# The last pair's queries and keys moved through DRAM in two parts

## The chip, the cores and the metric

The kernel runs on one core of a Trainium2 chip. The metric is the device time of one execution in microseconds (us), the median of several runs. TensorE (PE) does matmuls, VectorE (DVE), ScalarE (ACT) and GpSimd (POOL) the elementwise work, and nearly all DMAs are issued from the queue of SyncE (SP), in the order of that queue.

## The reference

Two layers on a sequence of 512 tokens with 1024 features, all in float32. Layer A (the one that the change touches) is a dilated sliding-window attention with three groups (dilation 1, 4 and 16), layer B a neighbourhood attention on a grid of 8 x 64 tokens.

```python
hn = rms_norm(x, norm_gain[i])
proj = hn @ w_in                          # q, k, v for 3 groups x 16 heads of 64, and a gate
...
    q = rms_norm(qkv[:, :, g, 0], q_gain[g])      # per head
    k = rms_norm(qkv[:, :, g, 1], k_gain[g])
    v = qkv[:, :, g, 2]
    o, lse = dilated_group_attention(q, k, v, t5_bias, dilation, reach)
...
alpha = jax.nn.softmax(jnp.stack(lses), axis=0)   # merges the three groups
y = jnp.sum(alpha[..., None] * jnp.stack(outs), axis=0) * jax.nn.silu(gate)
x = x + y @ w_out
```

## The kernel before, in words

**Tiling.** Work in a layer goes by pairs of heads, `hc` = 0 to 7. For each pair of layer A, `main_a` projects, with three float32r matmuls for each float32 product (weights and activations are split into a high and a low part: `wh`/`wl`, `hn_h`/`hn_l`):

- "rawk": dilated keys and values of groups 1 and 2 (keys normed into the last 256 of the 768 columns of each quarter of `rq`, called `rawq` in the trace);
- "rawq": three groups' queries and group 0's near keys (the first 512 columns of each quarter);
- group 0's values, and the gate.

For pairs 0 to 6 "rawk" comes first; for pair 7 "rawq" comes first, then "rawk", the gate of pair 6, the values and the gate of pair 7, and then the output product over all eight pairs (`out_product`, `acc<-y,wh` in the trace). Two pieces of weights (`wraw`, 512 KB each, four buffers) are loaded ahead by SP; ACT copies each into `wh` (L142), DVE or POOL makes `wl` (L150).

**How queries and keys are moved.** The scores need each head's 64 features on partitions, so every pair goes through a transposition: DVE norms (L336) and transposes 32x32 blocks in place (`turn_raw`, L591); `move_q` (L686) writes all 768 columns of the four quarters to a DRAM tile `qd` (1.5 MB, one DMA, L692), and four reads of 32 partitions each bring them back as `qt` (L699). Then `split_q` (L747) has ACT spread group 0's keys into `k0` (L753) and the queries of the three groups into places of their own (L750, L753). The dilated keys are used from `qt` directly. The scores (`log<-k,rawk` for group 0, `log<-qt,q` for the dilated groups, L238) follow, 16 and 32 matmuls for each of the four token blocks (two blocks in a half of the pair).

The scores of pair 6 that have gone through softmax make the same kind of trip (`tr` to `td` to `pt`: L882, L886), as do group 0's values (`vv` to `vd` to `vv`: L641, L645). The biases of a pair are loaded as `e` (L845).

**What sets the order.** PE's order is written out: `run` walks through `main` (projections and output product), and between its steps through `side` (attention), which yields delays in a modelled clock of PE's work (`clock`), in ns. `yield "wait", key, delay` lets `side` go on when the clock is `delay` past the moment at which `key` was stamped; `later_on(delay, job)` puts a job, often a DMA, at a later point of the same clock. So delays in the code are places in the program, not times on the chip: on the chip each engine runs its own list in order and waits for what an instruction needs. DMAs marked `keep_in_program_order` stand in SP's list where the clock put them. Each DMA on SP also takes one of eight semaphores in turn, so it waits for the landing of the one issued eight before it.

For pair 7, `q_a` (L680) waits for the "rawk" stamp and `Q7` = 9500, then calls `move_q`; `land` waits to `Q7` + 10000 and calls `split_q`; `attn_a` then yields 3500 and emits the first scores.

Of the kernel before, what the change touches and what calls it, by code (L numbers as in the profile page):

```python
# [13 lines left out]
F32 = mybir.dt.float32  # L14
# [8 lines left out]
P = 128  # L23
# [3 lines left out]
NHC = 8  # L27
# [4 lines left out]
EXT = S + 64  # L32
LINE = 384 + 2 * 448
W5 = 5 * 32
Q7 = 9500
RUN = 6 * 64
EB = 8 * W5

# [22 lines left out]
def tile_hybrid_encoder(  # L61
# [11 lines left out]
    nc = tc.nc  # L73
# [8 lines left out]
    dr = ctx.enter_context(tc.tile_pool(name="dr", bufs=1, space=DRAM))  # L82
# [29 lines left out]
    def slot(k, name, dtype):  # L112
        return big.tile([P, 2 * S], dtype, tag="y%d" % k, name=name)
# [137 lines left out]
    def later_on(delay, job):  # L251

        timers.append((clock[0] + delay, job))
        timers.sort(key=lambda t: t[0])
# [123 lines left out]
    def row_scale(ssq):  # L378

        rsqrt(nc.vector, rs_n, ssq, 4, 1.0 / D)  # L380
# [48 lines left out]
    def square_a(k):  # L429
        nc.scalar.activation(x_of(k), x_of(k), AF.Square)  # L430
# [72 lines left out]
    st = {}  # L503
    pq = wk.tile([P, 4096], F32, tag="pt", name="pt", bufs=1)
    rk = wk.tile([P, 4096], F32, tag="rawk", name="rawk", bufs=1)
    rq = wk.tile([P, 3072], F32, tag="rawq", name="rawq", bufs=1)
# [163 lines left out]
    def q_tiles(hc):  # L670


        if ("q", hc) not in st:
            st["q", hc] = (
                wk.tile([P, 4, 6, P], F32, tag="q12", name="qt", bufs=1),
                wk.tile([P, EXT], F32, tag="k0", name="k0", bufs=1),
            )
        return st["q", hc]

    def q_a(hc):  # L680

        yield "wait", *((("rawq", hc), 8000) if hc < NHC - 1 else (("rawk", hc), Q7))
        del st["rawq", hc]
        move_q(hc)

    def move_q(hc):  # L686

        d = dr.tile([4, P, 768], F32, name="qd", tag="qd", bufs=2)
        left = [4]

        def write():
            tc.keep_in_program_order(nc.sync.dma_start(d.rearrange("a p x -> p a x"), rq.rearrange("p (a x) -> p a x", a=4)))  # L692
            stamp["q", hc] = 0

        def read(a):
            qt, _ = q_tiles(hc)
            dst = qt[32 * a : 32 * a + 32].rearrange("k t f x -> k t (f x)")
            src = d[a].rearrange("(t k) x -> k t x", t=4)
            tc.keep_in_program_order(nc.sync.dma_start(dst, src))  # L699
            left[0] -= 1  # L700

        later_on(600, write)

        def land():
            for a in (0, 2, 1, 3):
                later_on(6500 if hc < NHC - 2 else 5000, partial(read, a))
            if hc < NHC - 1:
                yield "wait", ("rawk" if hc < NHC - 2 else "rawq", hc + 1), 0
            else:
                yield "wait", ("rawk", hc), Q7 + 10000  # L710
            assert not left[0]
            split_q(hc, *q_tiles(hc))
            yield

        st["land", hc] = land

# [24 lines left out]
    def split_q(hc, qt, k0):  # L741
        src = qt[:, :, 3, :].rearrange("p s (j i) -> p s i j", j=4)
        dst = k0[:, 64:EXT].rearrange("p (i s j) -> p s i j", s=4, j=4)
        tc.keep_in_program_order(scaled(dst, src, 0))
        both = slot(hc, "q12", F32)
        areas = st["areas", hc] = rk[:, 3072 : 3072 + S], both[:, :S], both[:, S:]
        for g, to in enumerate(areas):  # L747
            src = qt[:, :, g, :].rearrange("p s (x r) -> p s x r", r=8)
            dst = to.rearrange("p (x s r) -> p s x r", s=4, r=8)
            tc.keep_in_program_order(scaled(dst, src, g) if g else nc.scalar.copy(dst, src))  # L750

    def scaled(dst, src, g):
        return nc.scalar.activation(dst, src, AF.Copy, scale=gk[:, g : g + 1])  # L753
# [140 lines left out]
    def attn_a(hc):  # L894
# [115 lines left out]
        if hc < NHC - 1:  # L1010
            for u in range(2):
                if u == 0:
                    yield "wait", ("rawk" if hc < NHC - 2 else "rawq", hc + 1), 6500
                elif hc < NHC - 3:
                    yield "wait", ("open", hc + 1), 2500
                elif hc == NHC - 3:
                    yield "wait", ("rawq", hc + 1), 9000
                else:
                    yield "wait", ("rawq", hc + 1), 23200
                turned = turner(512)  # L1020
                turners.append(turned)
                for hd, t, pr in scores(u):
                    turned.put(pr, 512, 256 * hd + 64 * (t % 2), 128)
                send = partial(turned.send, pq[:, 2048 * u : 2048 * u + 2048], *((6000, 500) if u else (8500, 1200)))
                later_on(7000 + 2000 * u, send)
                if pending and u == 0:
                    yield 7500
                    pending.pop(0)()
                    yield 0
                if u == 0:  # L1030
                    yield "half"
            pending.append(lambda: put_y(hc, weigh(), True, False))
        else:
            for u in range(2):
                yield 3500 if u == 0 else 600
                held = scores(u)
                if u:
                    stamp["ya", "turned"] = 0
                yield 3200
                if pending:  # L1040
                    yield "wait", ("gate", hc - 1), 18500
                    pending.pop(0)()
                    yield
                for args in held:
                    turn_p(*args)
                    yield
            yield "wait", ("v", hc), 0
            put_y(hc, weigh(), True, True)
            stamp["ya", "last"] = 0
            yield  # L1050
# [271 lines left out]
    def side():  # L1322
        for k in range(KT):
            norm(0, k, x_of(k))
            if k:
                square_a(k - 1)
            stamp["na", k] = 0
            if k == 4:
                gains()
            yield 1000  # L1330
        square_a(KT - 1)
        for k in range(1, KT):
            yield 1300
            nc.vector.tensor_add(x_of(0), x_of(0), x_of(k))
        yield 1500
        row_scale(row_sums(x_of(0)))
        yield 2500
        bias_lines()
        later_on(21000, lambda: st.__setitem__(("e", 0), bias_a(0)))
        yield 2500  # L1340
        scales_a()
        first_out()
        stamp["rs", "a"] = 0
        halves = []
        for hc in range(NHC):
            if hc < NHC - 1:
                yield from q_a(hc)
                if hc:
                    yield from halves.pop(0)
                yield from st.pop(("land", hc))()  # L1350
                half = attn_a(hc)
                for v in half:
                    if v == "half":
                        if hc == 0:
                            later_on(12500, bias_rows)
                        if hc in (4, 5):
                            for n in range(2):
                                later_on(9000 + 3500 * n, st["rows"].pop())
                        halves.append(half)
                        break  # L1360
                    yield v
            else:
                gap[0] = cycle((500, 500, 700))
                yield from halves.pop(0)
                yield from q_a(hc)
                yield from st.pop(("land", hc))()
                yield from attn_a(hc)
        yield from residual(xg, 0)
        yield from residual(xg, 4)
        stamp["ya", KT - 1, "y"] = 0  # L1370
        yield "wait", ("x", KT - 1), 800
        for f in range(KT):
            square_b(f)
            yield 600
        yield 4500
        row_scale(row_sums(st.pop("ssq")))
        stamp["rs", "b"] = 0
        yield 5000
        nc.scalar.mul(rs_half, spread(), 0.5)
        stamp["rs", "all"] = 0  # L1380
        for job, hc, delay in B_PLAN:
            yield "wait", ("b", "start"), delay
            if job == "scores":
                yield from side_b(hc)
                continue
            if hc == NHC - 1:
                yield "wait", ("back", hc), 0
                yield from residual(xm_d, 0)
            yield "wait", ("back", hc), 3500
            if hc == NHC - 2:  # L1390
                stamp["yb", "turned"] = 0
            pending.pop(0)()
            if hc == NHC - 1:
                stamp["yb", "last"] = 0
            yield
            if hc == NHC - 1:
                yield from residual(xm_d, 4)
# [105 lines left out]
```

## Time and profile before

| | |
|---|---|
| median of 3 runs | 813.52 us (813.51 to 813.93) |
| the profiled execution | 815.16 us, span 813.4 us |
| busy, share of the span | PE 795.8 us (98%), DVE 531.3 (65%), ACT 444.4 (55%), POOL 221.2 (27%) |
| chain that ended last | PE 82%, DVE 8%, DMA 5%, ACT 2% |
| DMA | 178.43 MB, 219 GB/s on average |
| layer A's last pair | first scores at 512.43 us, output product from 490.25 us |

In the rows of the trace, times are us from the span's start. A row of a timeline has start, duration, engine, line of the code, operation, output <- inputs, and in brackets how long the engine was idle before it and what ended that. `wraw<-in_w` is a load of weights. "Granted clock" is the share of full speed that PE's throttle allowed; "DMA share" is the mean busy share of the core's 16 DMA engines.

### The profile page before, as it was taken

The page shows a single profiled execution, that of the slowest core. Times are in us where ns is not written, and L with a number is a line of the kernel's source. Part 1 is how long each engine was busy: PE and PEld are TensorE (multiplying, and loading weights), DVE is VectorE, ACT ScalarE, POOL GpSimd, SP SyncE. Part 2 cuts the span into 40 slices and gives each one's busy share as a digit, 9 for nine tenths or more (in the row PEclk, how much of TensorE's full clock was granted, in tenths as well). Part 3 has the DMA queues.
Part 4 walks back from the last instruction along what each step waited for, and adds up shares of the span by engine and source line. Part 5 has one row for each costly group of instructions (what it writes and reads, how often), then busy time and mean ns, then how long its engine had stood idle before and what let it go on. Part 6 is the DMA issues. An engine that isn't in the chain of part 4 may idle for free.

```text
span 813.4 us, 17707 instructions
## 1 busy us (share of the span) xinstructions
PE 795.8 (98%) x6690; PEld 652.2 (80%) x6690; DVE 531.3 (65%) x1409; ACT 444.4 (55%) x936; POOL 221.2 (27%) x349
## 2 busy tenths in 40 slices
PE   9999999999999999999999995799999999999998
PEld 7888888888888888888888884678888888878887
DVE  7474675675675675675676784348565788796844
ACT  7442745645645645744746662545535665657721
POOL 3242432332432432432433131111130405020010
PEclk9999999999999999999999999799999999999999
DMA  8579588878977987987978589327745797799564
GB/s 288 167 203 261 145 240 245 252 202 251 267 218 221 271 240 220 273 270 204 267 266 236 183 233 276 95 63 287 182 155 172 218 229 223 217 258 279 160 157 177
DMA packets 99590, 178.43 MB, mean 219 GB/s; under 512 B 16752, under 2 KB 53632, under 8 KB 99504
## 3 DMA queue, kind: packets, MB, share of 16 engines
q1 hardware_dynamic: 99360, 177.03, 74.4%
q8 instruction: 53, 0.87, 0.4%
q10 hardware_dynamic: 144, 0.26, 0.1%
q14 instruction: 33, 0.27, 0.1%
HBM read 132.82 MB, written 52.70 MB: 228 GB/s over the span
## 4 chain that ended last, share of the span: by engine, by line
PE 82%; DVE 8%; DMA 5%; ACT 2%; issue 1%; POOL 0%; SPq 0%; ACTq 0%; DVEq 0%; POOLq 0%
PE acc L238 73%; PE log L238 4%; PE o L238 4%; DMA wraw<-in_w 2%; DVE wl L150 1%; DVE rawq L336 1%; DMA qt<-qd 1%; DMA vv<-vd 1%; DMA qd<-rawq 1%; DMA vv<-bd 1%; DVE rawq L591 1%; PE busy L402 1%; DVE p L942 1%; ACT p L1262 0%; DVE na L129 0%
## 5 line engine op out<-in xcount | busy, mean ns | idle before, releaser
L238 PE MATMUL acc<-wh,hn_h 128*128 128x512 f32 x704 | 277.5, 395 | 0.0
L238 PE MATMUL acc<-wh,hn_l 128*128 128x512 f32 x704 | 273.7, 389 | 0.0
L238 PE MATMUL acc<-wl,hn_h 128*128 128x512 f32 x704 | 273.7, 389 | 0.0
L142 ACT CAST wh<-wraw 128x512 fp32r<-128x512 f32 (+1 forms) x257 | 157.2, 615 | 192.2 <-PE acc L238 165.2
L150 DVE TENSOR_TENSOR wl<-wraw,wh 128x512 fp32r<-128x512 f32 (+2 forms) x186 | 139.1, 749 | 142.0 <-ACT wh L142 140.2
L150 POOL TENSOR_TENSOR wl<-wraw,wh 128x512 fp32r<-128x512 f32 (+1 forms) x72 | 97.0, 1348 | 242.8 <-ACT wh L142 182.6
L238 PEld LDWEIGHTS acc<-wh,hn_h 128*128 128x128 f32 x704 | 132.4, 188 | 31.4 <-issue 3.8
L238 PEld LDWEIGHTS acc<-wh,hn_l 128*128 128x128 f32 x704 | 132.2, 188 | 28.0
L238 PEld LDWEIGHTS acc<-wl,hn_h 128*128 128x128 f32 x704 | 132.2, 188 | 26.8 <-POOL wl L150 0.3
L316 POOL TENSOR_TENSOR sq<-rawq 128x256 f32<-128x256 f32 (+1 forms) x80 | 57.7, 729 | 123.4 <-ACT rawq L554 109.8
L238 PE MATMUL acc<-y,wh 128*128 128x512 f32 (+1 forms) x272 | 82.6, 387 | 1.0 <-DVE mn L954 0.6
L965 ACT ACTIVATE p<-p,mn 128x512 f32<-128x512 f32 (+1 forms) x64 | 44.8, 702 | 60.6 <-DVE mn L954 60.6
L238 PE MATMUL acc<-hn_h,wh 128*128 128x512 f32 x192 | 75.4, 393 | 0.1
L238 PE MATMUL acc<-hn_h,wl 128*128 128x512 f32 x192 | 74.9, 390 | 0.0
L238 PE MATMUL acc<-hn_l,wh 128*128 128x512 f32 x192 | 74.8, 389 | 0.0
L317 DVE TENSOR_REDUCE ss<-sq 128x4 f32<-128x256 f32 (+1 forms) x96 | 47.7, 506 | 35.0 <-POOL sq L316 30.3
L238 PEld LDWEIGHTS acc<-y,wh 128*128 128x128 f32 x272 | 49.5, 190 | 11.0 <-PE log L238 0.8
L238 PE MATMUL acc<-y,wl 128*128 128x512 f32 (+1 forms) x136 | 51.7, 380 | 0.0
L336 DVE TENSOR_TENSOR rawq<-rawq,rs 128x256 f32<-128x256 f32 (+1 forms) x96 | 47.1, 551 | 2.5 <-POOL rs L134 2.2
L873 DVE STREAM_TRANSPOSE tr<-p 128x512 f32<-128x512 f32 x56 | 38.9, 706 | 11.9 <-ACT p L789 11.7
L554 ACT ACTIVATE rawq<-acc,rs_n 128x512 f32<-128x512 f32 (+1 forms) x76 | 46.1, 613 | 0.5
L789 ACT ACTIVATE p<-p,mn 128x512 f32<-128x512 f32 (+1 forms) x64 | 44.4, 701 | 2.4 <-DVE mn L788 2.3
(127 smaller groups left out, 908.0 us busy)
## 6 DMA issues: line engine op xcount, KB each, us to landing
wraw<-in_w SPq DMA_DIRECT2D x121, 512.0 KB, 5.6
td<-tr SPq DMA_DIRECT2D x14, 1024.0 KB, 7.4
pt<-td SPq DMA_DIRECT2D x56, 256.0 KB, 4.9
qd<-rawq SPq DMA_DIRECT2D x8, 1536.0 KB, 7.6
qt<-qd SPq DMA_DIRECT2D x32, 384.0 KB, 6.6
tdb<-tb SPq DMA_DIRECT2D x8, 768.0 KB, 6.1
pt<-tdb SPq DMA_DIRECT2D x32, 192.0 KB, 5.7
eb<-eb_d SPq DMA_DIRECT2D x32, 160.0 KB, 5.7
```

What stands on the lines that cost most here:

```text
L142: nc.scalar.copy(h, raw)
L150: eng.tensor_sub(l, raw, h.bitcast(F32))
L238: nc.tensor.matmul(o, l, r, **kw)
L316: nc.gpsimd.tensor_mul(to, v, v)
L317: nc.vector.tensor_reduce(ss[:, i * ns : (i + 1) * ns], sq.rearrange("p (a b) -> p a b", b=64), axis=AX.X, op=ALU.add)
L336: m = nc.vector.tensor_mul(v, v, by)
L402: nc.tensor.matmul(busy, wide(P), wide(S), start=True, stop=True)
L554: nc.scalar.activation(dst, src, AF.Copy, scale=rs_n[:, i : i + 1])
L591: tc.keep_in_program_order(nc.vector.transpose(x, x))
L789: nc.scalar.activation(pr, pr, AF.Copy, scale=mn[:, 3:4])
L873: nc.vector.transpose(dst, src[:, :n].rearrange(order, b=4, k=32, **({"g": 2} if apart else {})))
L965: nc.scalar.activation(row, row, AF.Exp, bias=mn[:, 1:2], scale=-1.0, accum_out=mn[:, 2:3])
```

## The change

For the last pair alone, `move_last` takes the place of `move_q`. The queries (and near keys), 512 of each quarter's 768 columns, are written when their own norm is through, read back in four reads after the next projection, and spread by `split_q` earlier. The dilated keys, 256 columns, are written and read back by themselves later: `Q7` is now 13000 and their reads stand 4500 behind that. The half-finished attention of pair 6 (`halves.pop(0)`) now runs after `q_a` of pair 7, and the pause ahead of the last pair's first scores is 6000 where it was 3500.

```diff
-Q7 = 9500
+Q7 = 13000
...
     def q_a(hc):
-        yield "wait", *((("rawq", hc), 8000) if hc < NHC - 1 else (("rawk", hc), Q7))
+        yield "wait", ("rawq", hc), 8000
         del st["rawq", hc]
-        move_q(hc)
+        (move_q if hc < NHC - 1 else move_last)(hc)
...
-            if hc < NHC - 1:
-                yield "wait", ("rawk" if hc < NHC - 2 else "rawq", hc + 1), 0
-            else:
-                yield "wait", ("rawk", hc), Q7 + 10000
+            yield "wait", ("rawk" if hc < NHC - 2 else "rawq", hc + 1), 0
...
+    def move_last(hc):
+
+        d = dr.tile([4, P, 768], F32, name="qd", tag="qd", bufs=2)
+        queries, keys = slice(0, 512), slice(512, 768)
+
+        def write(x):
+            src = rq.rearrange("p (a x) -> p a x", a=4)[:, :, x]
+            tc.keep_in_program_order(nc.sync.dma_start(d.rearrange("a p x -> p a x")[:, :, x], src))
+
+        def read(x):
+            for a in (0, 2, 1, 3):
+                dst = q_tiles(hc)[0][32 * a : 32 * a + 32].rearrange("k t f x -> k t (f x)")[:, :, x]
+                src = d[a].rearrange("(t k) x -> k t x", t=4)[:, :, x]
+                tc.keep_in_program_order(nc.sync.dma_start(dst, src))
+
+        later_on(600, partial(write, queries))
+
+        def land():
+            yield "wait", ("rawk", hc), 2000
+            read(queries)
+            yield "wait", ("rawk", hc), 12500
+            split_q(hc, *q_tiles(hc))
+            yield "wait", ("rawk", hc), Q7
+            write(keys)
+            yield "wait", ("rawk", hc), Q7 + 4500
+            read(keys)
...
-                yield 3500 if u == 0 else 600
+                yield 6000 if u == 0 else 600
...
                 gap[0] = cycle((500, 500, 700))
+                yield from q_a(hc)
                 yield from halves.pop(0)
-                yield from q_a(hc)
                 yield from st.pop(("land", hc))()
```

What this does to the engines' lists is shown at three places. In the changed kernel, line numbers behind the new function are 26 higher. `x4` means four such instructions in a row; sizes are partitions and elements.

First place, SP's list where pair 6's first half of scores goes out to DRAM (`td`), during pair 7's projections. Before:

```order
L882 DMA td<-tr 128x4x512
L845 DMA e_5442<-l_d 128x2x256
L845 DMA e_5443<-l_d 32x4x224 x4
L886 DMA pt<-td 32x4x512 x4
L202 DMA wraw<-in_w 128x1024 x2
```

And now:

```order
L908 DMA td<-tr 128x4x512
L721 DMA qd<-rawq 128x4x512
L871 DMA e_5444<-l_d 128x2x256
L871 DMA e_5445<-l_d 32x4x224 x4
L912 DMA pt<-td 32x4x512 x4
L202 DMA wraw<-in_w 128x1024
L727 DMA qt<-qd 32x4x512 x4
L202 DMA wraw<-in_w 128x1024
```

The queries' write stands right behind `td`, their four reads behind the first of the two loads of weights.

Second place, SP's list that follows, where pair 6's second half goes out and the keys of pair 7 are through their norm. Before:

```order
L882 DMA td<-tr 128x4x512
L202 DMA wraw<-in_w 128x512
L886 DMA pt<-td 32x4x512
L692 DMA qd<-rawq 128x4x768
L202 DMA wraw<-in_w 128x1024
L641 DMA vd<-vv 128x4x128
L202 DMA wraw<-in_w 128x768
L699 DMA qt<-qd 32x4x768 x4
L886 DMA pt<-td 32x4x512 x3
L645 DMA vv<-vd 32x4x128 x4
```

And now:

```order
L908 DMA td<-tr 128x4x512
L202 DMA wraw<-in_w 128x512
L721 DMA qd<-rawq 128x4x256
L912 DMA pt<-td 32x4x512 x4
L202 DMA wraw<-in_w 128x1024
L727 DMA qt<-qd 32x4x256 x4
L641 DMA vd<-vv 128x4x128
L202 DMA wraw<-in_w 128x768
L645 DMA vv<-vd 32x4x128 x4
```

The keys' write has moved ahead of all four `pt` reads (one stood before it, three behind the reads of `qt`); the keys' reads stand behind those four and one load of weights; the values' `vd` has moved behind the keys' reads.

Third place, ACT's list between the last two gates of layer A (`eg<-gt` is a gate's tanh, `gt<-acc` the copy of a gate out of PSUM) and the last pair's first softmax. Before:

```order
L613 ACTIVATE eg<-gt 128x512
L142 CAST wh<-wraw 128x512 x4
L608 COPY gt<-acc 128x512
L613 ACTIVATE eg<-gt 128x512
L142 CAST wh<-wraw 128x512 x3
L753 ACTIVATE k_5716<-qt,gk 128x4x32x4
L750 COPY rawk<-qt 128x4x16x8
L753 ACTIVATE q_5771<-qt,gk 128x4x16x8 x2
```

And now:

```order
L613 ACTIVATE eg<-gt 128x512
L142 CAST wh<-wraw 128x512 x2
L779 ACTIVATE k_5619<-qt,gk 128x4x32x4
L776 COPY rawk<-qt 128x4x16x8
L779 ACTIVATE q_5706<-qt,gk 128x4x16x8 x2
L142 CAST wh<-wraw 128x512 x2
L608 COPY gt<-acc 128x512
L613 ACTIVATE eg<-gt 128x512
L142 CAST wh<-wraw 128x512 x3
```

The four instructions of `split_q` have moved ahead of five casts of weights, the copy of pair 7's gate and its tanh. PE's list has the first scores at the same row as before; some transpositions of the last pair's softmax stand one group of three product matmuls earlier or later.

More of the change, by code (lines that the diff above doesn't have):

```diff
@@ L713, in land @@
             yield
+        st["land", hc] = land
+    def move_last(hc):
[19 more added lines that the diff above has]
+            read(keys)
         st["land", hc] = land
```

## The prediction

> **What bounds the kernel now.** I read the page first: TensorE (PE) is busy nearly all of the span and has most of the chain that ended last (both in the table above), so only its idle time and its slow-clock time can be won. The list of PE's waits names the one that matters:
>
> ```profile
> PE log L238 <- ACT rawk L750: 12.5, 1, 12.5
> ```
>
> All other PE waits there are below 1 us. The chain of waits around it (start, length, what) runs backwards from PE's scores of the last pair to DVE's transposition of its dilated keys:
>
> ```profile
> 489.42 1.30 DVE rawq L591 x2
> ...
> 491.72 7.93 DMA qd<-rawq
> ```
>
> So 1.5 MB of queries and keys went out to DRAM from 491.7 to 499.7, and only when they were read back could ScalarE (ACT) spread them. PE's timeline shows the price. The first two rows are the same scores one half-pair earlier at full clock, from the start of the 96 score matmuls to the start of what follows; then come one ordinary group of three product matmuls (494.33 to 495.01), the wait, and what ran behind it:
>
> ```profile
> 470.37 0.66 PE L238 MATMUL log<-k,rawk 64*32 64x256 f32 x16
> ...
> 472.21 0.50 PE L238 MATMUL acc<-wh,hn_h 128*128 128x512 f32 x1
> ...
> 494.33 0.62 PE L238 MATMUL acc<-y,wh 128*128 128x512 f32 x2
> 494.79 0.39 PE L238 MATMUL acc<-y,wl 128*128 128x512 f32 x1
> 495.01 0.62 PE L238 MATMUL acc<-y,wh 128*128 128x512 f32 x2
> ...
> 499.55 0.39 PE L238 MATMUL acc<-y,wl 128*128 128x512 f32 x1
> 512.43 0.89 PE L238 MATMUL log<-k,rawk 64*32 64x192 f32 x16 [12.50 <-ACT rawk L750]
> ...
> 515.99 1.22 PE L238 MATMUL acc<-y,wh 128*128 128x512 f32 x2
> ...
> 518.58 0.63 PE L238 MATMUL acc<-y,wh 128*128 128x512 f32 x2
> ```
>
> Busy time by stretch (after the engines' busy times stand granted clock, DMA share, GB/s) shows when the clock fell and rose:
>
> ```profile
> 504.00:506.00 2.00, 0.00 (x0) 0.00 (x0) 0.00 (x0) 0.00 (x0) 0.00 (x0) 0.69 1.05 221
> 518.00:520.00 2.00, 2.00 (x10) 1.59 (x9) 0.98 (x7) 1.81 (x6) 0.00 (x0) 0.90 0.00 0
> ```
>
> A mean of 0.69 between 1.0 and 0.5 puts the fall at 504.8, 4.8 us into the wait; 0.90 puts the rise at 518.4, 6 us after PE restarted. The scores took 3.56 us instead of 1.84 (1.72 lost), the next two groups of three 2.59 instead of 2 x 0.68 (1.23 lost). The stall costs 12.5 + 2.95 = 15.4 us in all, the most that the change can win.
>
> **The change part by part.** *What leaves the path.* The score matmuls stand at the same place in PE's order as before (the longer pause in the last pair's scores, 6000 for 3500, makes up for the earlier split), so PE arrives at 499.94 unless something ahead is late. ACT's spreading of queries and near keys (`split_q`) goes ahead; PE then does the first 16 near matmuls (some 0.4 us, as the 96 took 1.84 at full clock) and waits, from 500.4, for the dilated keys' reads alone, with no ACT work between landing and use. The gain is 15.4 us minus what is left of the wait, minus slow clock. All hangs on when the keys land.
>
> *The keys, if the queues were empty.* Their transposition ends at 490.72. Layer B moves pieces of exactly this shape, a 512 KB write and four 128 KB reads (the list of DMA issues: count, KB, median us to landing):
>
> ```profile
> bd<-rawq SPq DMA_DIRECT2D x8, 512.0 KB, 3.5
> ...
> rawq<-bd SPq DMA_DIRECT2D x16, 128.0 KB, 3.9
> ```
>
> 490.7 + 3.5, then four issues (the last begins some 1.3 us after the first) and 3.9 more, is 499.4 to 500. That is PE's arrival: the whole 15.4 us would be won. This is the lower bound.
>
> *The queues aren't empty.* SP's timeline has the issues (start, time in the sequencer):
>
> ```profile
> 468.30 0.38 SPq L882 DMA_DIRECT2D td<-tr  x1
> 468.73 3.95 SPq L845 DMA_DIRECT2D e<-l_d  x5
> 473.74 2.69 SPq L886 DMA_DIRECT2D pt<-td  x4
> 476.54 6.16 SPq L202 DMA_DIRECT2D wraw<-in_w  x2
> 486.09 0.38 SPq L882 DMA_DIRECT2D td<-tr  x1
> 486.88 0.33 SPq L202 DMA_DIRECT2D wraw<-in_w  x1
> ```
>
> and the DMA engines' load by stretch:
>
> ```profile
> 468.00:482.00 14.00, 14.00 (x150) 11.33 (x149) 10.64 (x31) 10.09 (x23) 5.71 (x10) 1.00 1.02 264
> 482.00:486.00 4.00, 4.00 (x19) 3.04 (x18) 3.93 (x11) 2.40 (x5) 1.73 (x2) 1.00 0.43 141
> 494.00:500.00 6.00, 5.94 (x27) 4.58 (x25) 3.32 (x5) 2.28 (x4) 1.29 (x1) 1.00 1.03 375
> 500.00:512.00 12.00, 0.00 (x0) 0.00 (x0) 0.00 (x0) 1.30 (x2) 0.00 (x0) 0.70 1.04 235
> ```
>
> The change puts the queries' write (1.05 MB) behind the `td` write of 468.30 and their four reads (1.05 MB) behind the first weight load of 476.54: 2.1 MB more in the stretch from 468 to 482, which is saturated already (share 1.02). The slack of 482 to 486 (share 0.43) takes part of it, and the rest pushes back all that follows. SP's new order puts four `pt` reads, which wait for the second `td` write to land, and a weight load between the keys' write and the keys' reads. Sizes by the shapes in the order, in MB: `td` 1.05, queries out 1.05, bias `e` 0.72, `pt` 1.05, weights 0.52, queries back 1.05, weights 0.52, `td` 1.05, weights 0.26, keys out 0.52, `pt` 1.05, weights 0.52, keys back 0.52: 9.88 MB. At 264 GB/s that is 37.4 us, from 468.3 to 505.7. The queue never runs dry under this sum: when SP issues the second `td` (486.1) it has work to 490.9, at the keys' write (490.7) to about 496. I add 0.8 us for the lag at both ends (chosen; the bd rows are mostly lag): the keys land at 506.5. I take 264 because that stretch holds the same mixture of writes, 32-partition reads and weight loads. The bounds are 375 GB/s (writes and weights alone), which ends before the empty-queue floor, so 500; and 235 (mostly 32-partition reads), 42.0 us, so 511.1.
>
> A rule of the Trainium skill speaks against the change: "DMA: Bandwidth & Descriptors", section "Rules for kernel authors", wants transfers of 1 MiB and more and small ones coalesced, and here four 384 KB reads become four of 256 and four of 128. If by it the key reads moved at half the rate (an estimate), their 0.52 MB would take 2 us more and the forecast below would be 807.7. The trace agrees in direction: the bd rows have a quarter of the bytes take no less time.
>
> *What PE loses then.* It waits from 500.4 to 506.5, 6.1 us. The clock fell 4.8 us into the wait before, so this one is just over; with 2.95 us for a fall and 0 for none I take 1.5. Loss 7.6, gain 15.4 - 7.6 = 7.8 us.
>
> The Trainium skill ("TensorE: Matmul & The Clock Gate", "What's actually happening") has a free-running window of 3.4 us that has to be idle as a whole; the trace agrees, since fall and rise lie 13.6 us, four windows, apart. By it a 6.1 us wait brings a fall in (6.1 - 3.4) / 3.4 = 0.8 of executions (an estimate), and the gain would be nearer 7.
>
> *The spreading on ACT.* ACT works in order. Its rows: the weight casts, the copy of the last gate, and the spreading as it is now:
>
> ```profile
> 487.30 1.65 ACT L142 CAST wh<-wraw 128x512 fp32r<-128x512 f32 x3
> ...
> 490.80 0.58 ACT L608 COPY gt<-acc 128x512 f32<-128x512 f32 x1
> ...
> 510.70 1.18 ACT L753 ACTIVATE k<-qt,gk 128x512 f32<-128x512 f32 x1 [11.64 <-DMA qt<-qd]
> ...
> 512.29 1.33 ACT L753 ACTIVATE q<-qt,gk 128x512 f32<-128x512 f32 x2
> ```
>
> The spreading takes 510.70 to 513.62, 2.9 us. It now stands behind two casts (done at 488.4), ahead of two more and of that gate's copy, which frees the PSUM bank of the product's fourth block; PE begins that block at 494.33. The queries land after 5.44 MB of the sum, 20.6 us, at 489 to 490. From 490: spreading to 492.9, two casts (0.55 each) to 494.0, copy to 494.6. PE loses 0.3 us there and takes it back out of its later wait. Each us that the queries land later costs PE one more there, free up to some 6 us; beyond that it counts.
>
> *Parts at nothing.* SP's added write and four added reads are five issues of about 0.4 us, hidden while the queue is the limit. The values' move (`vd`, `vv`) and later weight loads fall behind the keys, but are used only with the last pair's weighing and the next blocks. One transposition fewer or more between product groups on PE keeps the number of matmuls. If the cover is gone, each of these shows as a PE wait of well under 1 us, as the two there now.
>
> **The rivals.** *The queue is lighter than my sum* (mixed traffic above 283 GB/s): the keys land by 504, the wait is 0 to 3.6 us without slow clock, and 11.8 to 15.4 us are won, 798.1 to 801.7. For it speaks the 375 GB/s of 494 to 500 and the bd rows; against it that the `pt` reads can't start before `td` has landed. *The queue runs at the rate of reads*, 235 GB/s: keys at 511.1, wait 10.7, slow clock 2.95, gain 1.8, so 811.7; between this and the forecast lies the rest, 809.2 to 811.9. *Slower than before*: the queries' detour delays `td`, SP stands blocked before `pt`, and the keys land later than all of the data does now. The point is 500.4 + 12.45 = 512.9, reached if the 9.88 MB move at 226 GB/s or less; at 215 they take 46 us, the keys land at 515.1 and it takes 815.7. The 235 of the read stretch is near; but half of the bytes are writes and weights, which moved at up to 375. *The change does nothing measurable*: keys between 511.3 and 514.5, from the same sum at 218 to 234 GB/s.
>
> **How the numbers follow.** The profiled execution took 815.16 us with a span of 813.4; the median of the runs is 813.52, so the gain is taken off the median: 813.52 - 7.8 = 805.7. The forecast (keys from 504 without slow clock to 508.5 with it) spans 801.7 to 809.2 and gets 0.62; the light queue 0.17; the slow queue 0.11; no change 0.05; slower 0.05. About 0.2% (1.6 us) is what a measurement can tell from no change. Faster has 0.62 + 0.17 + 0.11 = 0.90. A range of 799.5 to 810.0 holds the forecast, two thirds of the light queue and a third of the slow one: 0.8.
>
> **What would show it.** Right: PE's wait at the last pair's first scores is released by a DMA (`qt<-qd`), not by ACT, and lasts 4 to 8 us; the queries are spread near 490 to 493; DMA share is near 1 without a break from 468 on; PE's clock dips later or not at all. Wrong: a wait under 2 us (my queue is too long), a new PE wait near 494 longer than 2 us (queries too late), or a wait of over 10 us there (the detour ate the gain).

## The result, and the profile after

The changed kernel takes 806.67 us (median of 4 runs, 805.29 to 807.72), beside 813.72 us for the kernel before on the same chip (4 runs, 813.51 to 814.52): a ratio of 0.991, 95% interval 0.9893 to 0.9928. The gain is 7.05 us; 7.8 was forecast. The profiled execution took 807.72 us with a span of 805.9, 7.5 less than the 813.4 of before.

First the list of PE's waits in the whole span (us in total, times, longest). The wait of 12.5 us for ACT's copy is gone and two shorter ones stand in its place:

```profile
PE acc L238 <- ACT gt L608: 3.1, 1, 3.1
PE log L238 <- DMA qt<-qd: 2.5, 1, 2.5
```

PE's timeline shows where they lie. The first is at the product's fourth block, the second between the near scores and the dilated ones. The last row is the first product group behind the last pair's weighing; the same instruction stood at 547.19 in the trace of before:

```profile
497.36 0.73 PE L238 MATMUL acc<-y,wh 128*128 128x512 f32 x2 [3.15 <-ACT gt L608]
...
503.05 0.56 PE L238 MATMUL log<-k,rawk 64*32 64x192 f32 x16
506.14 1.36 PE L238 MATMUL log<-qt,q 64*32 64x128 f32 x25 [2.54 <-DMA qt<-qd]
...
509.36 0.86 PE L238 MATMUL acc<-y,wh 128*128 128x512 f32 x2
510.06 0.39 PE L238 MATMUL acc<-y,wl 128*128 128x512 f32 x1
510.29 0.62 PE L238 MATMUL acc<-y,wh 128*128 128x512 f32 x2
...
538.79 0.73 PE L238 MATMUL acc<-y,wh 128*128 128x512 f32 x2
```

What is still lost at this place can be read off these rows. The two waits are 3.15 and 2.54 us. From 506.14 to 509.36 the other scores take 3.22 us; the prediction's full-clock rows give 1.84 for all 96, about 0.4 of it for the 16 that ran before, so 1.8 us are slow clock, and the group from 509.36 to 510.29 is 0.25 longer than the ordinary 0.68. Together 3.15 + 2.54 + 2.05 = 7.7 us, against 15.4 before.

At the weighing the changed kernel is 547.19 - 538.79 = 8.4 us ahead: 7.7 from this place, 0.32 that it was ahead already when the product began (489.93 for 490.25), and a wait of 0.61 us for DVE at 534.81 in the trace of before that is gone (8.6 in all, 0.2 over). Of the 8.4, 0.7 is given back in layer B between 654 and 742 us, where DVE's list stands in another order; 0.5 of it at 686.14, where PE waits for DVE (`gx`, L1210) as it didn't before. Why DVE is late there wasn't tried.

The queue's side is SP's timeline (start, time in the sequencer):

```profile
468.03 0.38 SPq L908 DMA_DIRECT2D td<-tr  x1
468.46 0.50 SPq L721 DMA_DIRECT2D qd<-rawq  x1
...
479.91 2.51 SPq L727 DMA_DIRECT2D qt<-qd  x4
483.43 0.36 SPq L202 DMA_DIRECT2D wraw<-in_w  x1
485.81 0.38 SPq L908 DMA_DIRECT2D td<-tr  x1
...
490.46 0.37 SPq L721 DMA_DIRECT2D qd<-rawq  x1
496.39 1.74 SPq L912 DMA_DIRECT2D pt<-td  x4
498.24 0.38 SPq L202 DMA_DIRECT2D wraw<-in_w  x1
498.66 1.85 SPq L727 DMA_DIRECT2D qt<-qd  x4
```

SP issues nothing for almost 6 us behind the keys' write of 490.46: it stands before the `pt` reads until the `td` write of 485.81 has landed, 10.6 us after its issue. The keys' reads stand behind these, but the block itself hardly delays them: the keys' write, from which they read, landed at 498.4, 8.0 us after its issue, and they go out at 498.66. ACT's timeline tells when the queries were back, and who held up the gate's copy that frees the fourth block's bank:

```profile
492.81 1.25 ACT L779 ACTIVATE k<-qt,gk 128x512 f32<-128x512 f32 x1 [4.68 <-DMA qt<-qd]
493.96 0.60 ACT L776 COPY rawk<-qt 128x512 f32<-128x512 f32 x1
494.47 1.33 ACT L779 ACTIVATE q<-qt,gk 128x512 f32<-128x512 f32 x2
495.70 1.12 ACT L142 CAST wh<-wraw 128x512 fp32r<-128x512 f32 x2
496.73 0.57 ACT L608 COPY gt<-acc 128x512 f32<-128x512 f32 x1
```

The DMA engines' load is in the last two numbers of these stretches (share, GB/s):

```profile
468.00:474.00 6.00, 6.00 (x115) 4.72 (x114) 4.20 (x6) 3.35 (x7) 3.33 (x5) 1.00 0.98 352
474.00:490.00 16.00, 16.00 (x72) 12.98 (x71) 14.25 (x47) 10.53 (x23) 4.10 (x6) 1.00 1.06 233
490.00:492.80 2.80, 2.80 (x14) 2.22 (x13) 2.29 (x5) 0.00 (x0) 0.00 (x0) 1.00 1.00 324
490.00:496.00 6.00, 4.21 (x19) 3.05 (x17) 2.29 (x5) 3.19 (x5) 0.00 (x0) 1.00 1.02 357
496.00:498.00 2.00, 0.64 (x3) 0.56 (x4) 1.14 (x1) 1.30 (x3) 1.49 (x2) 1.00 0.44 141
498.00:506.00 8.00, 5.60 (x39) 4.05 (x37) 4.18 (x7) 2.29 (x4) 1.35 (x2) 1.00 1.05 266
```

The engines are full from 468 on, but for the hole at 496 to 498 (share 0.44), where SP, held back until 496.4, is only starting on the `pt` reads.

### The profile page after: what moved, and what is told of

Same layout as the page of the kernel before. It is cut to its first block, busy times and chain, and to the rows that moved or that the text cites. A ratio compares the mean times of both kernels' runs of the same rounds, so it can differ in the third digit from the quotient of the medians.

```text
span 805.9 us, 17713 instructions
## 1 busy us (share of the span) xinstructions
PE 794.8 (99%) x6690; PEld 651.0 (81%) x6690; DVE 531.3 (66%) x1409; ACT 444.1 (55%) x936; POOL 221.3 (27%) x349
## 4 chain that ended last, share of the span: by engine, by line
PE 81%; DMA 7%; DVE 6%; ACT 3%; issue 1%; SPq 1%; POOL 0%; POOLq 0%; DVEq 0%; ACTq 0%
PE acc L238 73%; PE log L238 4%; PE o L238 3%; DMA qt<-qd 3%; DMA pt<-td 2%; ACT p L1288 1%; DMA td<-tr 1%; DVE rawq L336 1%; DVE wl L150 1%; DMA qd<-rawq 1%; SPq L871 1%; ACT wh L142 1%; ACT p L1293 1%; DMA x<-in_xt 0%; DMA wraw<-in_w 0%
```

## The experiments

Three theories stood at the start. The **queue theory**: the traffic ahead of them sets when the keys land, and what PE loses before that comes out of its last wait. The **chain theory**: norm, write and reads of the keys take their fixed time, whatever else is queued. The **spreading theory**: ACT's new place for the spreading is a loss of its own. All edits are on the changed kernel; the ratios are to the kernel before, measured on the same chip in the same session (medians 814.01 us for spread_late, keys_first, write_early and extra_load, 813.63 us for the other four).

### spread_late

```diff
-            yield "wait", ("rawk", hc), 12500
-            split_q(hc, *q_tiles(hc))
             yield "wait", ("rawk", hc), Q7
             write(keys)
             yield "wait", ("rawk", hc), Q7 + 4500
             read(keys)
+            split_q(hc, *q_tiles(hc))
```

> The spreading of the last pair's queries on ACT stands behind the gate's copy and the next weight casts (after the keys' reads in the program); SP's list is that of the changed kernel. Queue theory (the keys' landing is set by the traffic ahead of it, and all that PE loses earlier comes out of its last wait): PE's wait of 3.15 us at the product's fourth block goes, the wait at the scores grows from 2.5 to some 5.9 us and still ends when the keys land, near 506; total 806 to 807.5 us, ratio 0.990 to 0.992. Spreading theory (the place of the spreading on ACT is a loss of its own): 3 us less, 803.6 us, ratio 0.987.

It took 807.61 us (807.17 to 808.1), ratio 0.992 [0.9905, 0.9935]. PE's waits:

```profile
PE log L238 <- DMA qt<-qd: 3.6, 1, 3.6
PE acc L238 <- POOL wl L150: 1.5, 1, 1.5
```

The wait for the gate's copy is gone, a shorter one for weights came up, and the wait for the keys grew by 1.1 us, to 3.6 and not to the 5.9 expected: of the 3.1 us saved, 1.5 went into the new wait. In both kernels PE goes on 38.1 to 38.2 us after the first `td` write's issue (506.14 - 468.03 and 505.49 - 467.27). What PE saved ahead, it lost again before the keys were there; the whole is no faster than the changed kernel. The spreading theory falls. The 0.9 us by which it is slower lies within the spread of the runs.

### keys_first

```diff
+                pace = (11500 if hc == NHC - 2 else 6000, 500) if u else (8500, 1200)
-                send = partial(turned.send, pq[:, 2048 * u : 2048 * u + 2048], *((6000, 500) if u else (8500, 1200)))
+                send = partial(turned.send, pq[:, 2048 * u : 2048 * u + 2048], *pace)
```

This puts the four `pt` reads behind the keys' reads on SP.

> The four reads of pair 6's second half (pt, 1.05 MB) stand behind the keys' reads on SP instead of ahead of them. Queue theory: the keys' write still lands near 498.5, their reads then land at 502.5 to 503.5 instead of 506.0; the wait at the scores is 0 to 0.5 us, the clock does not fall, and 4 to 4.6 us go: 802 to 802.7 us, ratio 0.986. Chain theory (norm, write and reads of the keys have a fixed latency of some 15.5 us, whatever stands ahead): the keys land at 506 and the total stays at 806.7 us, ratio 0.991.

It took 803.37 us (802.11 to 805.58), ratio 0.9871 [0.9851, 0.989]. SP's timeline has the new order; the list of issues has how long the reads took (count, KB each, median us from issue to landing):

```profile
490.43 0.37 SPq L721 DMA_DIRECT2D qd<-rawq  x1
491.66 0.33 SPq L202 DMA_DIRECT2D wraw<-in_w  x1
498.21 1.74 SPq L727 DMA_DIRECT2D qt<-qd  x4
500.05 0.38 SPq L641 DMA_DIRECT2D vd<-vv  x1
500.48 1.96 SPq L912 DMA_DIRECT2D pt<-td  x4
```

```profile
qt<-qd SPq DMA_DIRECT2D x4, 128.0 KB, 2.6
```

The keys' write is issued when it was before, and the reads only 0.4 us sooner, but with 1.05 MB of `pt` no longer ahead of them they land in 2.6 us for 6.4. The last, issued at 499.5, is there at 502.2; in the changed kernel it was issued at 500.1 and there at 506.5. PE doesn't wait for it. The chain theory falls. Less was gained than expected, and the profiled execution was the slowest of the four. Its stretches show why (first number behind the PE entries: PE busy; granted clock third from the end):

```profile
493.00:494.00 1.00, 1.00 (x6) 0.63 (x4) 0.00 (x0) 1.00 (x2) 0.00 (x0) 1.00 1.06 412
494.00:495.00 1.00, 0.17 (x1) 0.00 (x0) 0.00 (x0) 1.00 (x2) 0.00 (x0) 1.00 1.08 403
...
496.00:497.00 1.00, 0.00 (x0) 0.00 (x0) 0.23 (x1) 1.00 (x3) 0.60 (x2) 0.56 1.08 419
...
502.00:503.00 1.00, 1.00 (x4) 0.72 (x4) 0.84 (x2) 0.00 (x0) 0.00 (x0) 0.53 0.81 239
```

The wait for the gate's copy is still there, and now the clock falls in it, at 496.1, and is back at 502.9. The near scores begin at 505.57 us, 2.5 later than in the changed kernel, although the wait ends at the same time.

### keys_first_filled

To tell the clock from the wait, the wait is filled with matmuls that compute nothing of use, into a spare bank. The order of the rest is that of keys_first.

```diff
                 yield from step(k, range(3), held[k])
+                if k == 1 and key == "ya":
+                    fill = bank("fill")
+                    for _ in range(13):
+                        nc.tensor.matmul(fill, wide(P), wide(S), start=True, stop=True)
```

> keys_first (803.37 us) with 13 matmuls that compute nothing of use, some 0.22 us each, put on TensorE where it waits for the gate's copy (494 to 497.3). They end before the copy does, so the wait's end stays at 497.3; only the clock can tell. Clock theory: the 3.1 us idle made the clock fall to half from 497.3 to about 503, and that cost 2.5 us; filled, the clock stays at 1, the near scores begin at 503.0 to 503.3 instead of 505.57, and it takes 800.5 to 801.5 us. Rival (the fall has another cause, or the order of the later work absorbs it): 803 to 804 us.

It took 802.94 us (802.71 to 803.3), ratio 0.9866 [0.9853, 0.988]. PE's timeline:

```profile
503.05 0.56 PE L238 MATMUL log<-k,rawk 64*32 64x192 f32 x16
503.40 0.69 PE L238 MATMUL log<-qt,q 64*32 64x128 f32 x32
```

In the profile the clock theory is met: the clock stays up, the scores begin at 503.05, and the span is 801.5 for 803.8. The time expected, 800.5 to 801.5, was missed: the medians differ by 0.4 us only, less than the spread of the runs, and not by 2 to 3. The expectation took the profiled execution of keys_first for a typical one. The runs list a mean clock each. In keys_first two runs had 1.000 (802.11 and 803.26 us), one 0.997 (803.48) and one 0.995 (805.58, the profiled one); with the wait filled, all four had 1.000, within 0.6 us of each other. So a wait of 3 us brings the fall in some executions, up to some 2.5 us each; how often, four runs don't tell.

### write_early

The queries' write goes out in the idle stretch ahead of 468 (462.94 instead of 468.46).

```diff
+        if key == "rawq" and hc == NHC - 1:
+            move_last(hc)
...
-        (move_q if hc < NHC - 1 else move_last)(hc)
+        if hc < NHC - 1:
+            move_q(hc)
...
-        later_on(600, partial(write, queries))
+        later_on(6000, partial(write, queries))
```

> The queries' write (1.05 MB) is issued at about 463.5, in the stretch from 460 to 466 in which the DMA engines move nothing, instead of at 468.5. Queue theory: all later traffic moves up by about 3 us: the queries land near 489.7 (was 492.8) and PE's wait at the fourth block shrinks from 3.15 to 0 to 0.5 us; the keys land near 503 (was 506.0), the wait at the scores is about 2.5 us without slow clock; total 801.5 to 803 us, ratio 0.985 to 0.987. Chain theory: the queries land earlier but the keys still at 506, PE waits 5.6 us at the scores; total 806 to 807 us, ratio 0.991.

It took 804.68 us (802.3 to 805.26), ratio 0.9874 [0.9854, 0.9894]. ACT's timeline and PE's list of waits:

```profile
489.51 1.28 ACT L782 ACTIVATE k<-qt,gk 128x512 f32<-128x512 f32 x1 [1.69 <-DMA qt<-qd]
```

```profile
PE log L238 <- DMA qt<-qd: 3.2, 1, 3.2
```

With 1.05 MB less in the stretch behind 468 the queries are back at 489.5 (492.8 in the changed kernel), 3.3 us earlier, and the fourth block doesn't wait. The keys land earlier too, PE going on 503.55 - 467.70 = 35.85 us after `td` for 38.11. But PE is also there sooner, and waits 3.2 us with the clock falling behind it (504.2 to 507.6), so the 801.5 to 803 us expected was missed. One of the four runs had a clock of 1.000, and took 802.3.

### extra_load

A useless copy of 0.52 MB, from DRAM to DRAM, is queued ahead of the keys' reads.

```diff
             yield "wait", ("rawk", hc), Q7 + 4500
+            extra = dr.tile([P, 1024], F32, name="extra")
+            tc.keep_in_program_order(nc.sync.dma_start(extra, w[:, :1024]))
             read(keys)
```

> A copy of 0.52 MB that nothing uses is issued right ahead of the keys' reads; the rest is the changed kernel. Queue theory: the keys land 1.4 us (at 375 GB/s) to 2.2 us (at 235 GB/s) later, at 507.4 to 508.2, and the total grows by as much, to 808.1 to 808.9 us, ratio 0.993 to 0.994. Chain theory: no change, 806.7 us, ratio 0.991.

It took 807.36 us (806.52 to 808.95), ratio 0.9919 [0.9903, 0.9935]. PE's waits:

```profile
PE log L238 <- DMA qt<-qd: 3.8, 1, 3.8
PE acc L238 <- ACT gt L608: 2.2, 1, 2.2
```

PE goes on after the keys 506.25 - 467.26 = 38.99 us after `td`, 0.9 later than in the changed kernel. The direction is the queue theory's, the size under half of the 2 us that 0.52 MB are worth at 264 GB/s. In the time the difference is within the spread of the runs, and the 808.1 to 808.9 us expected was not reached. This one is weak.

### one_move and one_move_first

The split is undone: one write and four reads of all 768 columns, and the spreading behind them. The change's other edits stay. one_move_first has the edit of keys_first as well.

```diff
-        queries, keys = slice(0, 512), slice(512, 768)
+        whole = slice(0, 768)
...
-        later_on(600, partial(write, queries))
 
         def land():
-            yield "wait", ("rawk", hc), 2000
-            read(queries)
-            yield "wait", ("rawk", hc), 12500
-            split_q(hc, *q_tiles(hc))
             yield "wait", ("rawk", hc), Q7
-            write(keys)
+            write(whole)
             yield "wait", ("rawk", hc), Q7 + 4500
-            read(keys)
+            read(whole)
+            split_q(hc, *q_tiles(hc))
```

> The split undone: all 768 columns, queries and keys, go out in one write and come back in four reads, 1.57 MB each way, behind the keys' norm at the place of the keys' write (the changed kernel's other edits, order of the halves and the pauses, are kept), and are spread behind that. Queue theory: out at 490.5 to about 497, pt and a weight load, then back; the same 9.88 MB as in the changed kernel, with the queue idle or half idle in 482 to 486, so all land at 507.5 to 510 and the spreading of the first keys and queries adds 1.2 to 2.5 us: scores at 509.5 to 512.5, with a slow clock, 811 to 813.5 us, ratio 0.997 to 0.9995. Rival (the other edits of the change brought the gain, not the split): 806 to 808 us.

> one_move with the pt reads put behind the keys' reads as in keys_first. Queue theory: the split matters less the lighter the queue is. From 490.5 only 1.57 MB out (375 GB/s and 2 us: 496.7), a weight load, and 1.57 MB back (near 240 GB/s and 2 us: 505.5 to 506.5), then 1.2 to 2.5 us of spreading: scores at 507 to 509, 808 to 810.5 us, ratio 0.993 to 0.996. It stays behind the changed kernel. Rival (the order on the queue is all that matters and the split nothing): 803 to 804.5 us, as keys_first.

one_move took 815.77 us (9 runs, 814.87 to 816.86), ratio 1.0023 [1.0014, 1.0033]: slower than the kernel before. one_move_first took 809.83 us (5 runs, 809.65 to 811.43), ratio 0.9955 [0.9941, 0.9968], as expected. The split is what gains: without it the other edits cost 2.1 us, and with the `pt` reads out of the way it is still worth some 6.5 (809.83 - 803.37, from two sessions). PE's waits and the reads' landing in one_move:

```profile
PE log L238 <- ACT rawk L771: 14.9, 1, 14.9
```

```profile
qt<-qd SPq DMA_DIRECT2D x4, 384.0 KB, 11.4
```

one_move was expected at 811 to 813.5, with all landed by 510. The reads were issued from 498.85 and landed up to 513.0. The expectation had counted the bytes ahead of the reads alone; weight loads and the values' write were issued while they ran, and by the sizes of the packets 0.85 MB of these had moved by 513.0, beside the reads. The prediction has the same error, below.

### both_moves

The edits of keys_first and write_early together.

> The early write of the queries and the keys ahead of the values' weights' (pt) reads, together. Queue theory: each cures one of the two waits of the changed kernel. The queries land near 489.5 as in write_early, so the wait for the gate's copy is gone; nothing but a weight load stands between the keys' write (490.4, landing in 5 to 6 us now that the queue is lighter) and the keys' reads (2.5 us in keys_first), so the keys land at 498.5 to 500.5 and PE's scores, due at 499.8, wait under 1 us; no fall of the clock. All of the 7.8 us lost in place come back, less the 0.7 given back in layer B: 798.0 to 800.0 us, ratio 0.981 to 0.983. Rival (some loss lies outside this place, or the pt reads, now last, hold up the weighing of the pair before): a new PE wait of over 2 us behind the scores, and 801.5 to 804.5 us, no better than either edit alone.

It took 800.14 us (799.68 to 800.65), ratio 0.9831 [0.9818, 0.9845], the best of all, 6.5 us below the changed kernel and just above the 798.0 to 800.0 expected. The reads of queries and keys land like those of write_early and keys_first; PE's timeline and its list of waits:

```profile
499.59 0.56 PE L238 MATMUL log<-k,rawk 64*32 64x192 f32 x16
499.94 0.69 PE L238 MATMUL log<-qt,q 64*32 64x128 f32 x32
```

```profile
PE acc L238 <- POOL y L858: 0.8, 1, 0.8
PE acc L238 <- DVE gx L1214: 0.4, 1, 0.4
```

The scores run without a wait at 499.59, and every run has a clock of 0.999 or 1.000. The span is 7.1 us shorter than that of the changed kernel, of the 7.7 us that were still lost there; a wait for POOL at 514.39 grew from 0.4 to 0.8.

## Why the prediction was right, and where it was wrong

**The gain and its place: right.** 805.7 us was forecast, 806.67 came. PE's wait is released by the keys' reads and no more by ACT, as said, and the loss left over is 7.7 us for 7.6. one_move shows that the split brings it. That the loss fits so well is partly luck: its waits are 0.4 us shorter and its slow clock 0.55 us longer than forecast, and more than half of the waiting stands at another place than forecast. By the prediction's own signs the wait at the scores, 2.5 us, lies below the 4 to 8 named for being right, the DMA share does break, at 496 to 498, and a new wait of 3.15 us near 494 is named as a sign of being wrong ("queries too late").

**The keys' landing: right, by two errors that cancel.** 506.5 was forecast; the last of the four reads landed at 506.5, the third, at which PE went on, at 506.0. The stretches of the changed kernel add up to 352 x 6 + 233 x 16 + 357 x 6 (490 to 496) + 141 x 2 + 266 x 8 = 10.4 MB in 38 us, 273 GB/s. The sum had 9.88 MB at 264: both 3 to 5% low. That the queue sets this landing is shown by keys_first (4.3 us earlier with 1.05 MB less ahead) and write_early (2.4 us earlier), both measured from `td` to the last read.

**"The queue never runs dry": wrong.** It half empties at 496 to 498, since SP stood before `pt` until 496.4. The prediction named that block as a rival's mechanism and put no price on it in the forecast.

**The queries' landing: the step that failed.** "The queries land after 5.44 MB of the sum ... at 489 to 490" took the queue for a strict line in which only what is ahead counts. They landed at 492.8. By then 352 x 6 + 233 x 16 + 324 x 2.8 = 6.7 MB had moved, 1.3 MB more. The sizes of the packets in the trace (4096 bytes for a weight load of 0.52 MB, 2048 for `td`) tell whose bytes these were: 0.28 MB belong to a weight load issued at 465.87, ahead of the sum, and about 1.0 to what SP issued while the queries' reads ran. Of the 0.52 MB of the weight load of 483.43, 0.51 had moved by 492.8, and of the `td` of 485.81 and the load behind it 0.48. They landed after the reads (at 493.9 and later) but moved beside them. So PE lost 3.15 us at the fourth block, not 0.3, and the chain of spreading, casts and copy from 492.8 on ran as worked out. The time shows nothing of it, for the reason that the prediction gave: up to some 6 us this comes out of the later wait. 3.15 + 2.54 = 5.7 us stand beside the 6.1 forecast, and spread_late, where the first wait is gone, is no faster. For the time it was this cover, and not a right sum, that saved the forecast.

**The slow clock: the right kind, 2.05 us for 1.5.** All four runs have a mean clock of 0.998, so the fall came in each. The prediction's second figure, a fall in 0.8 of executions and a gain nearer 7, came out closer than the 1.5: 7.05 us. But it was reached by luck: by its condition, a window idle as a whole, no fall was due here, since neither wait lasts 3.4 us. The last section shows what the falls went with.

**The rule on small transfers: not decided.** It would have made the keys' reads 2 us slower and the time 807.7 us; 806.67 lies midway between that and the forecast. In keys_first the four 128 KB reads land in 2.6 us each, 0.52 MB in 4.0 us from the first issue to the last landing, and in one_move_first the four of 384 KB in 6.3, 1.57 MB in 9.2 us: per byte the small ones were slower, but other traffic ran beside both. What made the keys' reads take 6.4 us in the changed kernel was mostly the traffic around them.

**The rivals.** The slower case and no change stayed away by far: the last of the keys landed 6.4 us ahead of the point of 512.9. The light queue is what keys_first and both_moves make on purpose; both_moves' 800.14 us lies in the 798.1 to 801.7 that were worked out for it.

## What to carry to other kernels

When data that are needed together are ready at different times, moving the early part early pays. On a full queue what is needed first has to be issued first: the `pt` reads ahead of the keys' reads cost some 3 us here (806.67 for 803.37), nearly all of it as bytes on the engines and only 0.4 us as time that SP stood blocked. Summing the bytes of a full queue at the rate of a stretch with the same mixture forecasts when the last of it lands (here bytes and rate came out 3 to 5% low, and the two errors cancelled); for an item in the middle, count what will be issued while it is under way, too. And read the clock of every run, not only of the profiled execution, before pricing a wait of a few us.

## What the runs showed of the hardware

The clock falls on less than a wholly idle window. In the changed kernel (stretches as above) it falls at 506.27 and is back at 509.68, 3.41 us later. In keys_first fall and rise lie 6.8 us apart, in the trace of before 13.6 (504.8 to 518.4): two and four times 3.41. The first three rows are of the changed kernel, the last two of keys_first, ahead of its fall and behind it:

```profile
502.86:506.27 3.41, 0.87 (x20) 0.32 (x18) 0.71 (x2) 0.00 (x0) 0.00 (x0) 1.00 1.11 283
...
506.00:506.50 0.50, 0.36 (x2) 0.14 (x2) 0.00 (x0) 0.00 (x0) 0.00 (x0) 0.77 1.19 407
...
509.50:510.00 0.50, 0.50 (x2) 0.46 (x3) 0.25 (x2) 0.50 (x3) 0.00 (x0) 0.82 0.76 172
...
492.70:496.12 3.42, 1.47 (x7) 0.89 (x5) 0.00 (x0) 3.39 (x5) 0.00 (x0) 1.00 1.06 396
496.12:499.53 3.41, 2.26 (x5) 1.82 (x6) 2.76 (x4) 1.16 (x4) 1.54 (x2) 0.50 0.54 209
```

The 3.41 us ahead of that fall hold 0.87 us of matmuls. In keys_first the fall is at 496.1, only 1.9 us after PE stopped (0.17 us into the stretch from 494), and the 3.41 us ahead of it hold some 1.5 us of matmuls; the clock is back at 502.9, two such windows later, the first of which was 2.3 us busy and brought no rise. So a window of 3.41 us that is more than half idle was enough to lower the clock, and one that is two thirds busy was not enough to raise it. Where between the two the limits lie, these runs don't tell.
